# A hybrid attention and long-convolution layer on one core: the short convolution's edge rows in two steps, with zero rows in DRAM, and the first long transform in the order of stored rows

## Chip, cores and metric

The kernel runs on one core of a Trainium2 chip. The metric is the device time of one execution in microseconds (us). The program is written in a tile framework: the Python code issues instructions in some order, a planner in the framework puts the instructions of each engine into a fixed order by priority and by its own estimate of when their inputs are ready (`schedule_with_timeline_sim=True`), and it adds all waits. Each engine, and each queue that issues transfers, then works through its list in order.

## What is computed

One encoder layer, run on two sequences of their own: `s` with 4096 tokens and `p` with 1024, width 1024. Half of the width goes through attention with three dilated windows, the other half through a gated long convolution of order two (hyena).

```python
proj = x @ w_in                              # q, k, v, g_attn: 512 each; u_h: 3 x 512; g_hyena: 512
attn = softmax-weighted sum of three dilated window attentions(q, k, v)
u = b + sum_j pad(u_h)[:, j:j + L] * w[j]    # short convolution, width 3, zero beyond both ends
z = u[..., :C]                               # C = 512
for n in range(2):
    gate = u[..., (n + 1) * C:(n + 2) * C]
    z = gate * (two_sided_fftconv(z, filters[n]) + d[n] * z)
mixed = [rms(attn) * silu(g_attn), rms(z) * silu(g_hyena)]
y = layer_norm(2 ** 0.25 * x + mixed @ w_out)
```

All of it is in float32. Matmuls are made from two-part operands (`h` and `l`, a rounded value and its rest), three products for one.

## The kernel before

Two chains of phases are woven together by `_interleave`. Each phase is a generator that yields the planned cost of the step it has just issued; the chain with the smaller sum goes next. A generator can also yield a name, a flag; its chain then waits until the name is in `self.done`.

- First chain: `proj_first` (u0, u1 and v from x, and x transposed), `proj_second` (u2, q, k), `attention` (which begins with `gate`, the attention's gate projection), `last`, `output`.
- Second chain: `filters` (the long filters and their first transform, into `G`), `convs` (the long convolutions), `hyena` (the hyena gate and the last step of the second convolution).

`proj_first` goes through 40 blocks of 128 tokens, 32 of `s` and 8 of `p`. Block r of a sequence holds the tokens a*R + r for a = 0 to 127, with R = L/128: 32 for `s`, 8 for `p`. So the neighbour of a token is mostly in the block before or after, on the same partition. `short_conv` (lines 416 to 448) takes the projection of one block from PSUM, multiplies it by the three taps, and adds to it what the block before has left. The finished row r - 1 of `u` goes to DRAM when block r is done. Rows 0 and R - 1 lack the contribution that crosses from one partition to the next. Their parts go to a scratch tensor `e` in DRAM (four parts of 128 x 512 for each of u0, u1, u2 of each sequence). A *wrap* finishes one such row: it clears a tile z (L440), loads 127 rows of `e`, shifted by one partition, into it (L441), loads the other part y (L442), adds them on GpSimd (L417) and stores the row of `u` (L444). There are two wraps for each u, twelve in all:

- the four of u0 and u1 of `s` are issued together at the end of block r = 0 of `p` in `proj_first`, then the flag `u_s` is set;
- the four of u0 and u1 of `p` together after the first block of `proj_second`, then the flag `u_p`;
- the two of u2 of `s` at the end of the `s` part of `proj_second`;
- the two of u2 of `p` one by one in `gate`, after steps 270 and 280.

In `proj_first` and `proj_second` the wraps take their two tiles from the tag `m2`, which the projections use too (three buffers in the first, MB = 4 in the second); in `gate` they take the tags kT and qT of attention's own loads.

`convs` runs, in this order: `conv_in(s)` (first transform of u0, into `X`), `conv_mid(s, 0)` (second transform, product with the filter, and back, into `B`), `conv_in(p)`, `conv_out(s)`, `conv_mid(p, 0)`, `conv_mid(s, 1)`, `conv_out(p)`, `conv_mid(p, 1)`. `conv_in` has NB/2 steps (NB = L/64: 32 steps for `s`, 8 for `p`); a step takes the rows n2 and n2 + 1 of `u[0]` seen as NB interleaved rows, in rising order of n2. Such a row n2 lies in the block row n2 mod R. `conv_mid` has NB steps. Its tiles fa and fi have two buffers each, z two, g three, x four. `conv_mid` reads all rows of `X` in every step, so it can't start before `conv_in` has finished.

Transfers are issued from SyncE's queue, all but a few constants (dz, mm, d1), which GpSimd issues. Lines that the prediction uses: L401 the projections' matmuls, L215 three-product matmuls, L478 the transposes of x (into xt; xn is the loaded x), L219 and L227 the rounding and the rest (xh, xl), L425 the stores of `u` and `e`, L663 the stores of `X`, L671 the loads of z in `conv_in`, L711 and L713 the result bo of a step of `conv_mid` and its store, L891 attention's scores, L486 the store of x transposed, L523 the store of v.

```python
m2 = tp.tile([P, C], F32, name="m2")         # a tile of a pool: same name, same ring of buffers
later.append(lambda tp, **k: wrap(tp, 0, slice(0, P - 1), 3, R - 1, **k))
later.append(lambda tp, **k: wrap(tp, 2, slice(1, P), 1, 0, **k))
```

Of the kernel before, what the change touches and what calls it, by code (L numbers as in the profile page):

```python
# [10 lines left out]
F32 = mybir.dt.float32  # L11
# [10 lines left out]
P = 128  # L22
D = 1024
C = 512
# [24 lines left out]
BOOT = 30  # L49
SEQS = (("s", 4096), ("p", 1024))  # L50
# [147 lines left out]
class _Kernel:  # L198
# [31 lines left out]
    def scratch(self, ctx):  # L230
        dp = self.pool(ctx, "dram", 1, DRAM)
        self.S = {}
        for nm, L in SEQS:
            NB = L // N1
            self.S[nm] = dict(
                L=L, NB=NB, A=L // 16,
                x=self.I["x_" + nm],
                R=L // P,
                u=[dp.tile([L, C], F32, name=f"u{i}_" + nm) for i in range(3)],
                e=[dp.tile([4, P, C], F32, name=f"e{i}_" + nm) for i in range(3)],  # L240
                qT=dp.tile([C, L], F32, name="qT_" + nm),
                kT=dp.tile([C, L], F32, name="kT_" + nm),
                v=dp.tile([L, H, VW], BF16, name="v_" + nm),
                o=dp.tile([3, L, H, 66], F32, name="o_" + nm),
                G=[dp.tile([2 * N1, NB, C], F32, name=f"G{i}_" + nm) for i in range(2)],
                X=[dp.tile([2 * N1, NB, C], F32, name=f"X{i}_" + nm) for i in range(2)],
                B=[dp.tile([2 * NB, N1, C], F32, name=f"B{i}_" + nm) for i in range(2)],
                xT=dp.tile([D, L], F32, name="xT_" + nm),
                ga=dp.tile([L, C], F32, name="ga_" + nm),
                mx=dp.tile([L, C], F32, name="mx_" + nm),  # L250
            )

    def globals_(self, ctx):
        nc = self.nc
        gp = self.pool(ctx, "one")
        self.ident = gp.tile([P, P], F32, name="ident")
        with self.tc.high_priority():
            nc.sync.dma_start(out=self.ident, in_=self.I["ident"])
        self.one = gp.tile([P, 1], F32, name="one")
        nc.vector.memset(self.one, 1.0)  # L260


    def filters(self, ctx):
# [151 lines left out]
    def short_conv(self, tp, w, st, nm, i, r, ps, later):  # L415
        nc, S = self.nc, self.S[nm]
        add = lambda o, x: nc.gpsimd.tensor_tensor(out=o, in0=o, in1=x, op=ALU.add)  # L417
        mul = lambda o, x: nc.vector.tensor_tensor(out=o, in0=ps, in1=x, op=ALU.mult)
        R, e = S["R"], S["e"][i]
        ur = S["u"][i].rearrange("(a r) c -> r a c", r=R)  # L420
        n2 = tp.tile([P, C], F32, name="m2")
        mul(n2, w[2])
        if r:
            nc.vector.tensor_tensor(out=n2, in0=n2, in1=st[i][0], op=ALU.add)
        nc.sync.dma_start(out=ur[r - 1] if r > 1 else e[r], in_=n2)  # L425
        t = tp.tile([P, C], F32, name="t0", bufs=3)
        mul(t, w[0])
        a = tp.tile([P, C], F32, name="acc", bufs=2)
        mul(a, w[1])
        add(a, st[i][1] if r else w[3])  # L430
        st[i] = (a, t)
        if r < R - 1:
            add(t, w[3])
            return
        nc.sync.dma_start(out=e[2], in_=t)
        nc.sync.dma_start(out=e[3], in_=a)

        def wrap(tp, src, dst, part, row, tags=("m2", "m2")):
            z, y = (tp.tile([P, C], F32, name=tag) for tag in tags)
            nc.vector.memset(z, 0.0)  # L440
            nc.sync.dma_start(out=z[dst], in_=e[src][slice(1, P) if dst.start == 0 else slice(0, P - 1)])  # L441
            nc.sync.dma_start(out=y, in_=e[part])  # L442
            add(y, z)
            nc.sync.dma_start(out=ur[row], in_=y)  # L444

        later.append(lambda tp, **k: wrap(tp, 0, slice(0, P - 1), 3, R - 1, **k))
        later.append(lambda tp, **k: wrap(tp, 2, slice(1, P), 1, 0, **k))


    def proj_first(self, ctx):  # L450
        nc = self.nc
        xp = self.pool(ctx, "a_x")
        xtp = self.pool(ctx, "a_xt")
        tp = self.pool(ctx, "a_t", 3)
# [4 lines left out]
        work = [(nm, r) for nm, L in SEQS for r in range(L // P)]  # L459
# [39 lines left out]
        st, later = {}, []  # L499
        for b, (nm, r) in enumerate(work):  # L500
            S = self.S[nm]
            for ci in range(3):
# [7 lines left out]
                if ci < 2:  # L510
# [11 lines left out]
                nc.gpsimd.tensor_tensor(out=v2, in0=r1, in1=v1, op=ALU.subtract)  # L522
                nc.sync.dma_start(out=S["v"].rearrange("(a r) h c -> r a (h c)", r=S["R"])[r],  # L523
                                  in_=vt.rearrange("p h c -> p (h c)"))
                if r == 0 and later:
                    for f in later:
                        f(tp)
                    self.done.add("u_" + work[b - 1][0])
                    later.clear()
                yield 5.3  # L530
            cur, nxt = nxt, []
        self.later = later


    def proj_second(self, ctx):
        nc = self.nc
# [36 lines left out]
        for b, (nm, g) in enumerate(work):  # L573
# [11 lines left out]
            for c2 in (2, 3, 0, 1):  # L585
# [24 lines left out]
                        with self.tc.high_priority():  # L610
                            nc.sync.dma_start(out=dst[:, :, c0:c0 + P], in_=qs[:, :, e * P:(e + 1) * P])
                yield 5.3
            if b == 0:
                for f in self.later:
                    f(tp)
                self.done.add("u_" + SEQS[-1][0])
            if last and b < len(work) - 1:
                for f in later:
                    f(tp)
                later.clear()  # L620
            self.later = later
            cur, nxt = nxt, []

        self.done.add("qk")
# [6 lines left out]
    def convs(self, ctx):  # L631
        self.ct = self.pool(ctx, "c_t", 2)
        self.cp = self.pool(ctx, "c_ps", 1, PSUM)
        a, b = (nm for nm, _ in SEQS)
        yield "u_" + a
        yield from self.conv_in(a)
        yield from self.conv_mid(a, 0)
        yield "u_" + b
        yield from self.conv_in(b)
        yield from self.conv_out(a)  # L640
        yield from self.conv_mid(b, 0)
        yield from self.conv_mid(a, 1)
        yield from self.conv_out(b)
        yield from self.conv_mid(b, 1)
        yield "qk"

    def slot(self, name, bufs=2, dt=F32):
# [17 lines left out]
    def conv_in(self, nm):  # L665
        nc, S = self.nc, self.S[nm]
        zr = S["u"][0].rearrange("(m n) c -> n m c", n=S["NB"])
        for n2 in range(0, S["NB"], 2):
            z = self.slot("z", ZB)
            for j in range(2):  # L670
                nc.sync.dma_start(out=z[64 * j:64 * j + 64], in_=zr[n2 + j])  # L671
            self.conv_dft(nm, 0, n2, z)
            yield 2.0

    def conv_mid(self, nm, n):
        nc, S, tp, pp = self.nc, self.S[nm], self.ct, self.cp
        NB = S["NB"]
# [3 lines left out]
        xf = S["X"][n].rearrange("k n c -> (k n) c")  # L681
        gf = S["G"][n].rearrange("k n c -> (k n) c")
        for s in range(NB):
            x = self.slot("x", XB)
            nc.sync.dma_start(out=x, in_=xf[s * P:(s + 1) * P])
            g = self.slot("g", GB)
# [80 lines left out]
    def attention(self, ctx):  # L767
# [79 lines left out]
        with ExitStack() as gx:  # L847
            for i, v in enumerate(self.gate(gx)):
                if i % BOOT == BOOT // 2 and i // BOOT < 9:
                    if i > BOOT:  # L850
                        self.lead = self.last_g
                    load(True)
                    self.lead = None
                if i >= 9 * BOOT and i % 10 == 0 and self.later:
                    self.later.pop(0)(lp, tags=("kT", "qT"))
                yield v
        sp = self.pool(ctx, "t_s", 2)
        pp = self.pool(ctx, "t_ps", 1, PSUM)
# [535 lines left out]
```

## Time and profile before

| | |
|---|---|
| runs | 4416.1, 4419.52, 4421.64 us; median 4419.52 |
| profiled execution | 4421.58 us, span 4419.8 us |
| TensorE matmul | 4038.2 us busy, 91% of the span |
| TensorE weight load | 3416.6 us, 77% |
| VectorE | 3218.0 us, 73% |
| ScalarE | 2152.8 us, 49% |
| GpSimd | 2003.6 us, 45% |
| DMA | 800.87 MB moved, 181 GB/s on average over 16 DMA engines |
| granted TensorE clock, mean | 0.96 |

The profile is of one execution. Its lines give the start and length of an instruction in us, the engine (PE is TensorE's matmul, PEld its weight load, DVE VectorE, ACT ScalarE, POOL GpSimd, SP SyncE; SPq is SyncE's queue, where a long row is an issue that waited), the line of the code, and what is written from what, by the names of tiles (a name like `e_s` is that of a DRAM tensor with its sequence; m is the tile m2, as trailing numbers are left out). In brackets stands how long the engine had been idle and what released it. Rows by stretches give, for one stretch of time, the busy us of each engine with its number of instructions, the granted clock as a share of full speed, the mean busy share of the DMA engines, and GB/s. Rows of groups give the busy us and the mean ns of one instruction, then the idle time ahead of them.

### The profile page before, as it was taken

Reading aid. Unit: us, or ns where it says so; the run is one execution under the profiler, and the core shown is the slowest. Engines: PE = TensorE matmul, PEld = TensorE weight load, DVE = VectorE, ACT = ScalarE, POOL = GpSimd, SP = SyncE. Lnnn points to the kernel's source line nnn. Section 1 sums busy time; section 2 is a strip of 40 time slices with the busy share of each in tenths; the row PEclk is TensorE's granted clock in tenths of the full one; section 3 lists DMA queues with packets and bytes.
Section 4 is the critical chain, followed back from the end, with each engine's and each line's share of the span. In section 5 each row is a group of like instructions: output and inputs, shape, how many; then the busy total and the mean of one; then the engine's idle time right before and its main releaser. Section 6 shows DMA issues by size and latency. Waiting matters only on the chain.

```text
span 4419.8 us, 87947 instructions
## 1 busy us (share of the span) xinstructions
PE 4038.2 (91%) x31996; PEld 3416.6 (77%) x31996; DVE 3218.0 (73%) x6503; ACT 2152.8 (49%) x4246; POOL 2003.6 (45%) x1714
## 2 busy tenths in 40 slices
PE   7999999868789999998989979999999999689897
PEld 6999999858579876887867647888888887477776
DVE  7889888447678754575788666878787877677774
ACT  3433334245344444443465446777777776223332
POOL 4444444335567731366655251414141432266664
PEclk9999999979899999999989988999999999799999
DMA  5555555579555579754566665656565556644441
GB/s 182 180 179 171 178 171 176 178 223 284 166 162 165 165 253 285 230 160 142 170 211 195 215 205 152 175 154 170 155 180 153 153 159 176 217 169 173 173 173 67
DMA packets 662475, 800.87 MB, mean 181 GB/s; under 512 B 68024, under 2 KB 400014, under 8 KB 662042
## 3 DMA queue, kind: packets, MB, share of 16 engines
q1 hardware_dynamic: 643610, 762.64, 55.4%
q0 software_dynamic: 18432, 32.60, 3.2%
q8 instruction: 254, 4.16, 0.4%
q14 instruction: 179, 1.47, 0.1%
HBM read 499.22 MB, written 295.80 MB: 180 GB/s over the span
## 4 chain that ended last, share of the span: by engine, by line
PE 55%; DMA 13%; DVE 10%; POOL 7%; issue 6%; ACT 3%; SPq 2%; POOLq 0%; DVEq 0%; ACTq 0%
PE qk L401 10%; PE u L401 10%; PE pv L950 6%; PE sc L891 5%; PE pt L924 4%; PE g L1182 4%; PE g L1131 3%; POOL hh L1309 2%; DMA oo<-o_s 2%; POOL oo L1271 2%; PE pf L215 2%; PE g L215 2%; PE pz L215 2%; PE c L735 1%; PE c L215 1%
## 5 line engine op out<-in xcount | busy, mean ns | idle before, releaser
L223 POOL TENSOR_SCALAR qc<-q 128x256 fp32r<-128x256 f32 x352 | 246.9, 719 | 707.6 <-PE sc L891 702.0
L401 PE MATMUL u<-wuh,xh 128*128 128x256 f32 x1920 | 556.2, 290 | 10.0 <-ACT wuh L219 9.2
L401 PE MATMUL u<-wul,xh 128*128 128x256 f32 x1920 | 549.1, 286 | 2.2 <-DVE wul L227 2.0
L401 PE MATMUL u<-wuh,xl 128*128 128x256 f32 x1920 | 547.7, 285 | 2.1 <-DVE xl L227 2.1
L227 DVE TENSOR_TENSOR x<-x,xh 128x512 fp32r<-128x512 f32 x320 | 357.7, 1140 | 248.4 <-ACT xh L219 245.6
L915 ACT ACTIVATE sb<-sb,ob 128x192 f32<-128x192 f32 (+2 forms) x960 | 412.2, 473 | 39.9 <-DVE ob L906 31.3
L401 PEld LDWEIGHTS u<-wuh,xh 128*128 128x128 f32 x1920 | 371.6, 194 | 22.8 <-ACT wuh L219 10.4
L401 PEld LDWEIGHTS u<-wul,xh 128*128 128x128 f32 x1920 | 371.8, 194 | 11.9 <-DVE wul L227 3.0
L401 PEld LDWEIGHTS u<-wuh,xl 128*128 128x128 f32 x1920 | 371.4, 193 | 9.9 <-DVE xl L227 2.9
L401 PE MATMUL qk<-xh,wql 128*128 128x256 f32 x1280 | 364.2, 285 | 0.7 <-DVE wql L227 0.5
L401 PE MATMUL qk<-xh,wqh 128*128 128x256 f32 x1280 | 364.4, 285 | 0.0
L401 PE MATMUL qk<-x,wqh 128*128 128x256 f32 x1280 | 364.2, 285 | 0.0
L927 ACT ACTIVATE th<-pt 96x512 f16<-96x512 f32 (+2 forms) x480 | 272.1, 576 | 177.7 <-PE pt L924 174.8
L950 PE MATMUL pv<-V,th 128*128 128x64 bf16 (+3 forms) x5568 | 334.8, 194 | 0.0
L950 PE MATMUL pv<-V,tl 128*128 128x64 bf16 (+3 forms) x3712 | 324.5, 195 | 8.5 <-DVE tl L935 5.4
L935 DVE TENSOR_TENSOR tl<-pt,th 96x512 f16<-96x512 f32 (+2 forms) x480 | 316.2, 667 | 18.8 <-ACT th L927 16.6
L704 POOL TENSOR_TENSOR z<-fa,fi 128x512 f32<-128x512 f32 x160 | 246.2, 1539 | 151.2 <-DVE fi L703 150.5
L227 POOL TENSOR_TENSOR g<-g,gh 128x512 fp32r<-128x512 f32 x160 | 221.1, 1383 | 183.0 <-ACT gh L219 171.4
L219 ACT ACTIVATE xh<-x 128x512 fp32r<-128x512 f32 x400 | 241.9, 633 | 127.4 <-DMA x<-xT_s 42.2
L950 PEld LDWEIGHTS <-th 128*128 128x128 f16 (+1 forms) x5568 | 291.5, 98 | 2.2 <-issue 2.2
L950 PEld LDWEIGHTS <-tl 128*128 128x128 f16 (+1 forms) x3712 | 252.1, 98 | 51.1 <-DVE tl L935 17.6
L924 PE MATMUL pt<-ident,sb 128*128 128x128 f32 (+1 forms) x1856 | 291.1, 283 | 0.3 <-DVE tl L935 0.3
(223 smaller groups left out, 12021.5 us busy)
## 6 DMA issues: line engine op xcount, KB each, us to landing
G_s<-go SPq DMA_DIRECT2D x128, 256.0 KB
g<-G_s SPq DMA_DIRECT2D x128, 256.0 KB
x<-X_s SPq DMA_DIRECT2D x128, 256.0 KB
B_s<-bo SPq DMA_DIRECT2D x128, 256.0 KB
x<-xT_s SPq DMA_DIRECT2D x64, 512.0 KB
oo<-o_s SPq DMA_DIRECT2D x32, 792.0 KB
u_s<-m SPq DMA_DIRECT2D x96, 256.0 KB
V<-v_s SPq DMA_DIRECT2D x168, 145.5 KB
```

The source lines that it names most:

```text
L215: nc.tensor.matmul(out=out, lhsT=l, rhs=r, start=(i == 0), stop=(i == n - 1))
L219: self.nc.scalar.activation(out, in_, AF.Copy, scale=scale)
L223: self.nc.gpsimd.tensor_scalar(out=out, in0=in_, scalar1=scale, scalar2=0.0, op0=ALU.mult, op1=ALU.add)
L227: e.tensor_tensor(out=out, in0=in_, in1=hi.bitcast(F32), op=ALU.subtract)
L401: nc.tensor.matmul(out=out, lhsT=l, rhs=r, start=(k == 0 and i == 0), stop=(k == len(pairs) - 1 and i == len(ops) - 1))
L704: nc.gpsimd.tensor_tensor(out=z, in0=fa, in1=fi, op=ALU.add)
L891: nc.tensor.matmul(out=st["sc"][i], lhsT=qv[half, x], rhs=f(y)[half], start=(j == 0), stop=(j == 2))
L915: nc.scalar.activation(sb[:, i, 0:W], sb[:, i, 0:W], AF.Exp, bias=st["ob"][:, ui, i, 65:66], scale=-1.0)
L924: nc.tensor.transpose(out=pt[0:n, i, t], in_=st["pr"][:, i, t * n:(t + 1) * n], identity=self.ident)
L927: nc.scalar.activation(th[0:n, :, 0:nkt], pt[0:n, :, 0:nkt], AF.Copy)
L935: e.tensor_tensor(out=tl[0:n, :, 0:nkt], in0=pt[0:n, :, 0:nkt], in1=th[0:n, :, 0:nkt], op=ALU.subtract)
L950: last = nc.tensor.matmul(out=pv[:, 0:w], lhsT=st[p][0:n, i, t], rhs=vv[:, VC[b]:VC[b] + w], start=(t == 0 and j == 0), stop=(t == nkt - 1 ...
```

## The change

- `e` gets two more rows in each part, one ahead of and one behind the 128. At the very start a zero tile of 128 x 4 is written to twelve rows of 512 floats in DRAM: the row behind part 0 and the row ahead of part 2, for each of three u and two sequences. The shifted load of a wrap is then 128 whole rows, one of them the zero row, and the clearing of the tile goes.
- A wrap has two steps: `begin` issues the two loads, `end` the add and the store. `wrap_step` first issues the `end` of the wrap begun before, then the `begin` of the next one.
- The four wraps of u0 and u1 of `s` go one by one after blocks r = 0 to 4 of `p` in `proj_first`, with tags of their own (wz, wy, one buffer each). The flag `w_s` is set after block 4.
- All later wraps are taken by whichever comes first, a step of `conv_mid` (tiles from the rings fa and fi) or, in `gate`, every tenth step from 270 on. The flag `w_p` is set by `conv_mid`.
- `conv_in` goes through its rows in the order in which they are stored: first those that need no wrap, each when the flag of its block is set (`u_s4` and so on), then the last four steps, which need `w_s` or `w_p`. The flags `u_s` and `u_p` go.

```diff
@@ -237,7 +237,7 @@
                 x=self.I["x_" + nm],
                 R=L // P,
                 u=[dp.tile([L, C], F32, name=f"u{i}_" + nm) for i in range(3)],
-                e=[dp.tile([4, P, C], F32, name=f"e{i}_" + nm) for i in range(3)],
+                e=[dp.tile([4, P + 2, C], F32, name=f"e{i}_" + nm) for i in range(3)],
                 qT=dp.tile([C, L], F32, name="qT_" + nm),
                 kT=dp.tile([C, L], F32, name="kT_" + nm),
                 v=dp.tile([L, H, VW], BF16, name="v_" + nm),
@@ -258,6 +258,13 @@
             nc.sync.dma_start(out=self.ident, in_=self.I["ident"])
         self.one = gp.tile([P, 1], F32, name="one")
         nc.vector.memset(self.one, 1.0)
+        zero = gp.tile([P, C // P], F32, name="zero")
+        nc.vector.memset(zero, 0.0)
+        for nm, _ in SEQS:
+            for e in self.S[nm]["e"]:
+                for k, row in ((0, P + 1), (2, 0)):
+                    nc.sync.dma_start(out=e[k, row].rearrange("(p f) -> p f", p=P), in_=zero)
+        self.wraps, self.adds = [], []
 
 
     def filters(self, ctx):
@@ -416,7 +423,7 @@
         nc, S = self.nc, self.S[nm]
         add = lambda o, x: nc.gpsimd.tensor_tensor(out=o, in0=o, in1=x, op=ALU.add)
         mul = lambda o, x: nc.vector.tensor_tensor(out=o, in0=ps, in1=x, op=ALU.mult)
-        R, e = S["R"], S["e"][i]
+        R, e = S["R"], [S["e"][i][k, 1:P + 1] for k in range(4)]
         ur = S["u"][i].rearrange("(a r) c -> r a c", r=R)
         n2 = tp.tile([P, C], F32, name="m2")
         mul(n2, w[2])
@@ -435,16 +442,27 @@
         nc.sync.dma_start(out=e[2], in_=t)
         nc.sync.dma_start(out=e[3], in_=a)
 
-        def wrap(tp, src, dst, part, row, tags=("m2", "m2")):
-            z, y = (tp.tile([P, C], F32, name=tag) for tag in tags)
-            nc.vector.memset(z, 0.0)
-            nc.sync.dma_start(out=z[dst], in_=e[src][slice(1, P) if dst.start == 0 else slice(0, P - 1)])
-            nc.sync.dma_start(out=y, in_=e[part])
-            add(y, z)
-            nc.sync.dma_start(out=ur[row], in_=y)
-
-        later.append(lambda tp, **k: wrap(tp, 0, slice(0, P - 1), 3, R - 1, **k))
-        later.append(lambda tp, **k: wrap(tp, 2, slice(1, P), 1, 0, **k))
+        def wrap(src, part, row):
+            def begin(tp, tags, **kw):
+                z, y = (tp.tile([P, C], F32, name=tag, **kw) for tag in tags)
+                nc.sync.dma_start(out=z, in_=src)
+                nc.sync.dma_start(out=y, in_=e[part])
+
+                def end():
+                    add(y, z)
+                    nc.sync.dma_start(out=ur[row], in_=y)
+                return end
+            return begin
+
+        later.append(wrap(S["e"][i][0, 2:P + 2], 3, R - 1))
+        later.append(wrap(S["e"][i][2, 0:P], 1, 0))
+
+    def wrap_step(self, *args, **kw):
+        for f in self.adds:
+            f()
+        self.adds = [f(*args, **kw) for f in self.wraps[:1]]
+        self.wraps = self.wraps[1:]
+        return not self.adds
 
 
     def proj_first(self, ctx):
@@ -522,14 +540,13 @@
                 nc.gpsimd.tensor_tensor(out=v2, in0=r1, in1=v1, op=ALU.subtract)
                 nc.sync.dma_start(out=S["v"].rearrange("(a r) h c -> r a (h c)", r=S["R"])[r],
                                   in_=vt.rearrange("p h c -> p (h c)"))
-                if r == 0 and later:
-                    for f in later:
-                        f(tp)
-                    self.done.add("u_" + work[b - 1][0])
-                    later.clear()
+                if nm != SEQS[0][0] and "w_" + SEQS[0][0] not in self.done and self.wrap_step(tp, ("wz", "wy"), bufs=1):
+                    self.done.add("w_" + SEQS[0][0])
+                if r == S["R"] - 1:
+                    self.wraps, later = later, []
+                self.done.add(f"u_{nm}{r}")
                 yield 5.3
             cur, nxt = nxt, []
-        self.later = later
 
 
     def proj_second(self, ctx):
@@ -610,15 +627,8 @@
                         with self.tc.high_priority():
                             nc.sync.dma_start(out=dst[:, :, c0:c0 + P], in_=qs[:, :, e * P:(e + 1) * P])
                 yield 5.3
-            if b == 0:
-                for f in self.later:
-                    f(tp)
-                self.done.add("u_" + SEQS[-1][0])
-            if last and b < len(work) - 1:
-                for f in later:
-                    f(tp)
-                later.clear()
-            self.later = later
+            if last:
+                self.wraps, later = later, []
             cur, nxt = nxt, []
 
         self.done.add("qk")
@@ -632,16 +642,17 @@
         self.ct = self.pool(ctx, "c_t", 2)
         self.cp = self.pool(ctx, "c_ps", 1, PSUM)
         a, b = (nm for nm, _ in SEQS)
-        yield "u_" + a
         yield from self.conv_in(a)
         yield from self.conv_mid(a, 0)
-        yield "u_" + b
         yield from self.conv_in(b)
         yield from self.conv_out(a)
         yield from self.conv_mid(b, 0)
         yield from self.conv_mid(a, 1)
         yield from self.conv_out(b)
         yield from self.conv_mid(b, 1)
+        for f in self.adds:
+            f()
+        self.adds = []
         yield "qk"
 
     def slot(self, name, bufs=2, dt=F32):
@@ -665,7 +676,12 @@
     def conv_in(self, nm):
         nc, S = self.nc, self.S[nm]
         zr = S["u"][0].rearrange("(m n) c -> n m c", n=S["NB"])
-        for n2 in range(0, S["NB"], 2):
+        R, NB = S["R"], S["NB"]
+        steps = [(f"u_{nm}{r + 2}", n2) for r in range(2, R - 2, 2) for n2 in (r, r + R)]
+        steps += [("w_" + nm, n2) for n2 in (R - 2, NB - 2, 0, R)]
+        for flag, n2 in steps:
+            if flag not in self.done:
+                yield flag
             z = self.slot("z", ZB)
             for j in range(2):
                 nc.sync.dma_start(out=z[64 * j:64 * j + 64], in_=zr[n2 + j])
@@ -681,6 +697,8 @@
         xf = S["X"][n].rearrange("k n c -> (k n) c")
         gf = S["G"][n].rearrange("k n c -> (k n) c")
         for s in range(NB):
+            if self.wrap_step(self.ct, ("fa", "fi"), bufs=2) and f"u_{SEQS[-1][0]}{self.S[SEQS[-1][0]]['R'] - 1}" in self.done:
+                self.done.add("w_" + SEQS[-1][0])
             x = self.slot("x", XB)
             nc.sync.dma_start(out=x, in_=xf[s * P:(s + 1) * P])
             g = self.slot("g", GB)
@@ -851,8 +869,8 @@
                         self.lead = self.last_g
                     load(True)
                     self.lead = None
-                if i >= 9 * BOOT and i % 10 == 0 and self.later:
-                    self.later.pop(0)(lp, tags=("kT", "qT"))
+                if i >= 9 * BOOT and i % 10 == 0:
+                    self.wrap_step(lp, ("kT", "qT"))
                 yield v
         sp = self.pool(ctx, "t_s", 2)
         pp = self.pool(ctx, "t_ps", 1, PSUM)
```

## Prediction

> **What bounds the kernel now.** I read the page first, for the busy shares and the slices, then busy time by stretches wherever the slices dip, then the chain of waits and the queues in order of time inside each dip.
>
> ```profile
> PE 4038.2 (91%) x31996; PEld 3416.6 (77%) x31996; DVE 3218.0 (73%) x6503; ACT 2152.8 (49%) x4246; POOL 2003.6 (45%) x1714
> PE   7999999868789999998989979999999999689897
> ```
>
> TensorE is busy 91% of the span; the next engine, VectorE, 73%. So the time is TensorE's work plus its holes, and a change that moves no matmul can win only in holes. One slice is 110.5 us; there are dips at slices 8 to 11 (884 to 1326 us) and around slices 18 to 23 (1990 to 2650 us). In the first dip SyncE's queue and VectorE, in order of time, show this:
>
> ```profile
> 863.47 3.46 SPq L442 DMA_DIRECT2D m<-e_s  x1
> 867.03 0.54 SPq L523 DMA_DIRECT2D v_p<-vt  x1
> 867.66 0.24 SPq L441 DMA_DIRECT2D m<-e_s  x1
> 878.16 0.33 SPq L444 DMA_DIRECT2D u_s<-m  x1
> ```
>
> ```profile
> 888.85 0.48 DVE L440 MEMSET m<- 128x512 f32 x1 [24.93 <-DMA u_s<-m]
> 889.25 0.63 DVE L227 TENSOR_TENSOR xl<-xt,xh 128x512 fp32r<-128x512 f32 x1
> 903.71 0.48 DVE L440 MEMSET m<- 128x512 f32 x1 [13.83 <-DMA u_s<-m]
> ```
>
> ```profile
> 907.58 1.22 PE L215 MATMUL pz<-gh,dz 128*128 128x512 f32 x2 [35.22 <-DVE gh L227]
> 920.65 0.79 PE L215 MATMUL pz<-gh,dz 128*128 128x512 f32 x1 [11.86 <-ACT fa L662]
> ```
>
> These are the four wraps of the long sequence's u0 and u1: each is a clearing of a tile (L440), two loads from the edge scratch e (L441, L442), an add and a store (L444). They share the tag m2 with the projection's own tiles, so the third and fourth clearing stand on VectorE until an earlier store has landed (24.93 and 13.83 us), and the split xl of the next projection block stands behind them. TensorE gets nothing for 35.22 and again 11.86 us. The chain of waits gives the price of one link:
>
> ```profile
> 867.66 10.50 DMA m<-e_s
> 878.16 10.44 DMA u_s<-m
> ```
>
> Why a 256 KB transfer takes 10 us shows in the DMA rates of another wrap (forty slices of 1985 to 2015 us):
>
> ```profile
> GB/s 224 19 14 22 27 25 25 27 25 27 25 25 27 25 25 27 25 25 87 325 270 142 276 290 385 57 25 25 25 25 27 25 25 25 16 248 385 339 183 377
> ...
> m<-e_s SPq DMA_DIRECT2D x1, 254.0 KB
> ```
>
> For some 10 us the whole core moves 25 GB/s, and then 300. The 254.0 KB load is the L441 one, 127 rows in place of 128: 254 KB / 25 GB/s = 10.2 us. Whole 256 KB transfers show no such plateau, so the 127-row load gets one lane of many, and stores issued behind it finish only after it. By the instructions of line 441 there are 6 + 4 + 2 = 12 of them:
>
> ```profile
> L441 SPq DMA_DIRECT2D m<-e_s x6: 242/247/3702, 862.2 to 1984.7; - x6
> L441 SPq DMA_DIRECT2D m<-e_p x4: 243/268/3652, 1167.3 to 1209.0; - x4
> L441 SPq DMA_DIRECT2D kT<-e_p x2: 242/244/245, 2503.9 to 2529.0; - x2
> ```
>
> They lie in four holes: A at 868 us (four), B at 1168 (four), C at 1988 (two), D at 2510 (two). Busy time by stretches, hole and neighbour:
>
> ```profile
> 868.00:922.00 54.00, 6.92 (x42) 5.80 (x41) 4.77 (x9) 4.08 (x7) 5.60 (x6) 0.57 0.27 85
> 922.00:942.00 20.00, 18.29 (x112) 16.46 (x112) 13.44 (x19) 12.21 (x22) 11.30 (x11) 0.81 0.84 271
> 940.00:1060.00 120.00, 112.04 (x819) 106.33 (x817) 87.82 (x105) 71.26 (x128) 56.53 (x61) 0.98 0.98 302
> 846.00:1085.00 239.00, 181.39 (x1308) 171.41 (x1308) 125.80 (x157) 97.88 (x173) 90.26 (x95) 0.87 0.74 230
> ```
>
> ```profile
> 1168.00:1230.00 62.00, 27.00 (x111) 22.50 (x110) 21.50 (x31) 9.85 (x19) 22.42 (x17) 0.70 0.31 106
> 1240.00:1320.00 80.00, 78.41 (x470) 69.30 (x469) 61.87 (x75) 39.08 (x70) 56.02 (x41) 1.00 0.53 168
> 1988.00:2014.00 26.00, 8.63 (x35) 6.70 (x34) 4.39 (x7) 2.27 (x4) 5.87 (x5) 0.70 0.31 101
> 1970.00:1990.00 20.00, 20.00 (x117) 17.55 (x116) 16.12 (x22) 10.54 (x19) 8.69 (x6) 1.00 0.49 163
> 2510.00:2560.00 50.00, 34.54 (x119) 20.56 (x118) 16.06 (x24) 15.67 (x28) 4.88 (x7) 0.86 0.74 238
> 2480.00:2510.00 30.00, 30.00 (x128) 21.72 (x126) 17.09 (x25) 14.23 (x25) 4.77 (x5) 1.00 0.75 228
> ```
>
> The columns are TensorE, weight load, VectorE, ScalarE and GpSimd busy us (with counts), then granted clock, DMA share, GB/s. I price a hole by its matmuls at the neighbour's pace, since busy time inside a hole counts matmuls at half clock.
>
> **The change, part by part.**
>
> *The wraps' loads become 128 whole rows, the clearing goes, and add and store move to the next step.* Nothing is left on VectorE (12 clearings of 0.48 us; VectorE has room), the slow lane is gone, and tiles have their own tags. I take all four holes as closed.
> A: 54 − 42/(819/120) = 47.9 us; and 922 to 942 us, where the clock is only 0.81, gives 20 − 112/6.83 = 3.6.
> B: 62 − 111/(470/80) = 43.1.
> C: 26 − 35/(117/20) = 20.0.
> D: 50 − 119/(128/30) = 22.1.
> Sum 136.7 us.
> The Trainium skill ("TensorE: Matmul & The Clock Gate", Part 1) says that after an idle window the clock stays at half for about one window of 3.4 us: by that the restart after A costs an estimated 1.7 us, and the sum would be 1.9 us smaller. The row's 0.57 and 0.81 agree in kind; I keep the row's 3.6.
>
> *Conv work starts earlier.* The first transform of the long sequence no longer waits for its wraps: 28 of its 32 steps touch stored rows only. Its loads start at the place of block r=0 of the short sequence (846 us) and not behind hole A. The last four need w_s, given at block r=4. The stretch 846 to 1085 holds eight blocks: (239 − 51)/8 = 23.5 us each, so 28 steps at the old pace (32 in about seven blocks) end near block six: the flag is no new wait. DMA is what is late next: 98% busy at 302 GB/s from 940 to 1060. The stretch moves 239 us × 230 GB/s = 55 MB, at 302 GB/s 182 us, against the 188 us left: just enough, so A's gain stands, with no room beyond it. The conv chain is then about one block, 23 us, ahead of the projections. That pays at the end of the gate, since attention starts only when the conv chain ends:
>
> ```profile
> 2662.38 0.79 PE L215 MATMUL c<-yl,mm 128*128 128x512 f32 x1
> 2663.10 0.53 PE L891 MATMUL sc<-kh,q 64*128 64x192 f32 x2
> ```
>
> Conv steps counted by line 711, in 1240 to 1560 us beside projections, and in 2590 to 2660 alone, with TensorE there:
>
> ```profile
> L711 ACT ACTIVATE bo<-c 128x512 f32<-128x512 f32 x46 | 27.0, 587 | 3.1 <-PE c L215 2.5 <-DMA u_s<-m 0.5
> ```
>
> ```profile
> L711 ACT ACTIVATE bo<-c 128x512 f32<-128x512 f32 x15 | 8.9, 596 | 4.4 <-PE c L215 3.6 <-DMA x<-X_p 0.5
> ```
>
> ```profile
> 2590.00:2660.00 70.00, 45.47 (x123) 24.98 (x121) 52.27 (x69) 37.19 (x65) 55.92 (x43) 0.83 0.63 176
> 0.00:40.00 40.00, 16.01 (x59) 12.10 (x60) 16.46 (x29) 16.92 (x26) 13.68 (x27) 1.00 0.90 287
> ```
>
> A step takes 320/46 = 7.0 us in company, 70/15 = 4.7 alone, and some 2 us of TensorE (8 to 9 matmuls). 23/7.0 = 3.3 steps leave the tail and cost 2 us each elsewhere: 3.3 × 2.7 = 9 us gained. Bounds 0 (nothing shifts) and 40 (all 15 steps: 70 − 30); I take 9.
>
> *New waits.* A wrap's second load may go only when the previous wrap's store has landed (wz and wy have one buffer), and it waits on SyncE's queue; behind it stand the next xn, z and X transfers of that stage, in the mid steps x, g and B. Without the slow lane a transfer's wait in this stretch is:
>
> ```profile
> 977.95 5.40 DMA z<-u_s
> ...
> 1067.11 3.66 DMA X_s<-fi
> ```
>
> Eight of the twelve wraps have a predecessor in their ring: 8 × 4.5 = 36 us if nothing covered it, 0 if the two-deep z and xn buffers do. I take 8, near the cover. In mid steps a wrap borrows one of the two fa and one of the two fi buffers for about eight steps; a step is 7 us and an fa is read within its own step, so 0 to 10 us: I take 3.
>
> *Twelve zero rows at the start.* Each is 128 pieces of 16 bytes, so 96 pieces on each of 16 lanes, in a stretch where DMA is 0.90 busy and TensorE waits for weights. A 2 KB row on the slow lane takes 10.2/127 = 0.08 us; at that price 96 take 7.7 us, at the other end 0, if small pieces are as cheap as those already there, between 3 and 40 us:
>
> ```profile
> DMA packets 7008, 11.32 MB, mean 306 GB/s; under 512 B 1182, under 2 KB 2292, under 8 KB 7008
> ```
>
> I take 4. The Trainium skill ("DMA: Bandwidth & Descriptors", Specifications) says that writes below 512 B are read, modified and written back. No run here shows one; as a doubling of the row's price, by my estimate, that is 15 us, and the sum would give 4302.
>
> Sum: −136.7 − 9 + 8 + 3 + 4 = −131. The profiled execution took 4421.6 us (span 4419.8), 2 us above the median of the runs: 4421.6 − 131 = 4291.
>
> **The rivals.**
>
> 1. *The wait moves to SyncE's queue.* The same eight holds are uncovered, each 4.5 us and a slow restart of 3.6: 65 us in place of 8, 4348. For it: the stretch is DMA-bound, so landings are slowest there, and every load and store of both chains is on this one queue. Against: z and xn are two deep, x four.
> 2. *The tail goes entirely.* If the conv chain gains 100 us on the projections in place of 23, 40 us are won for 9: 4260. For it: conv steps are far behind their place, 15 of them alone at the end. Against: TensorE is full between the holes, so the planner has no free place for them.
> 3. *Slower, by the zero rows.* They stand ahead of the weights at the start. They decide from 131/96 = 1.4 us for one 16-byte write on a lane; at 1.5 us the time is 4291 − 4 + 144 = 4431. Against: 17 times the row's price for 2 KB, and 1182 small pieces pass beside 306 GB/s.
> 4. *It doesn't do what it says:* the shifted load of 128 rows still goes at 25 GB/s, the adds and stores wait for it as before and only the clearing is off VectorE: about 4420. Against: L442's loads of the same scratch are whole and show no plateau of their own.
>
> **How the numbers follow.** The sum's case 0.66, rival 1 0.17, rival 2 0.08, rival 3 0.04, rival 4 0.05. A change under 0.2% can't be told from none. Faster: 0.66 + 0.17 + 0.08 = 0.91; same 0.05; slower 0.04. The likeliest's own range is 4265 (no new costs, 20 us from the tail) to 4330 (36 us of holds, 7.7 at the start, 10 in the rings). The range for 8 in 10 goes from 4255, under rival 2, to 4360, over rival 1.
>
> **What would show it.** Right: no stretch of 25 GB/s at the wraps; line 440's clearing gone and xl no longer behind it; TensorE's longest idle between 840 and 1250 us under 10 us; first attention matmul near 2663 − 137 − 9 = 2517 us; TensorE busy time near 4038 less the half-clock parts. Wrong: SyncE rows of several us at the wraps' second load, with TensorE idle behind; a first projection matmul later by over 10 us; conv steps alone before attention for more than 70 us, which would mean that the flag at block four holds the chain.

## The result, and the profile after

The changed kernel took 4301.41 us (median of 4 runs, 4298.37 to 4310.77) against 4417.81 us (4 runs) for the kernel before: ratio 0.9741, 95% interval 0.9722 to 0.9760. The forecast was 4291, range 4255 to 4360. The profiled execution took 4300.97 us, its span is 4299.2 us, 120.6 us shorter than the span before; the medians differ by 116.4, as the profiled execution before was among its slowest. All times here are those of executions at the usual clock; one of `e4_old_order`, 5736.61 us at a granted clock of 0.627, is left out.

Engine shares and slices from the page of the changed kernel:

```profile
PE 4010.9 (93%) x31996; PEld 3403.2 (79%) x31996; DVE 3210.6 (75%) x6492; ACT 2156.7 (50%) x4246; POOL 1998.5 (46%) x1714
PE   6999999998999999999899879999999998689987
```

The same 31996 matmuls; TensorE is busy 27 us less, at a mean granted clock of 0.971 in place of 0.96. The dip at slices 8 to 11 is gone. The DMA rates around the first four wraps (forty slices of 852 to 932 us), and the wraps' second loads:

```profile
GB/s 140 203 267 285 357 261 284 356 368 303 320 329 318 389 401 362 390 304 345 391 371 318 345 293 417 253 356 341 290 372 334 177 280 381 400 327 365 344 297 358
```

```profile
L449 SPq DMA_DIRECT2D wy<-e_s x4: 325/523/617, 856.5 to 912.6; - x4
L449 SPq DMA_DIRECT2D fi<-e_s x2: 319/351/383, 2446.4 to 2459.1; - x2
```

No plateau at 25 GB/s, and no issue of a wrap's second load took longer than 0.617 us (duration in ns, least, median, greatest): SyncE's queue did not stand there. TensorE's longest idle time between 840 and 1250 us is 4.5 us, before 35.2. Busy time where the holes were, and in the stretch before attention (columns as before):

```profile
852.00:1018.00 166.00, 164.91 (x1252) 158.08 (x1251) 118.81 (x143) 95.39 (x167) 86.95 (x93) 1.00 1.00 317
1120.00:1160.00 40.00, 38.69 (x257) 35.05 (x255) 28.99 (x35) 16.80 (x31) 31.46 (x24) 1.00 0.75 237
2370.00:2400.00 30.00, 27.57 (x112) 20.54 (x111) 14.51 (x21) 10.86 (x19) 7.96 (x7) 0.94 0.75 223
2448.00:2538.00 90.00, 54.12 (x141) 30.05 (x140) 58.61 (x81) 43.20 (x76) 66.83 (x51) 0.78 0.65 184
```

The first three are the places of the wraps of u0 and u1 of `s`, of `p`, and of u2 of `p`: TensorE is busy 99, 97 and 92%, in the first with the DMA engines full. The two wraps of u2 of `s`, before at 1988 us, are now issued at the head of the fourth stretch (2446.4 and 2459.1 us in the rows above). This stretch is the *tail*, from the gate's last store to attention's first score: TensorE does conv steps alone there, is 60% busy at clock 0.78, and the tail is longer than before. Where the 120.6 us come from is read from a few rows, first and last start of each group (the row that begins with a time is the issue of the first loads of `conv_mid(p, 1)`, the conv chain's last phase):

```profile
L342 SPq DMA_DIRECT2D G_p<-go x32: 319/320/455, 705.9 to 852.5; - x32
L703 SPq DMA_DIRECT2D x<-X_s x128: 319/382/1516, 1017.9 to 2329.2; - x128
L703 SPq DMA_DIRECT2D x<-X_p x32: 319/366/630, 1717.4 to 2508.3; - x32
2450.76 0.79 SPq L703 DMA_DIRECT2D x<-X_p  x2
L1158 SPq DMA_DIRECT2D ga_p<-wst x8: 319/320/473, 2397.7 to 2448.4; - x8
L909 PE MATMUL sc<-kh,q x512: 245/293/580, 2538.8 to 3257.6; 64*128 64x256 f32 x160, 64*128 64x192 f32 x11
```

Their like before:

```profile
L335 SPq DMA_DIRECT2D G_p<-go x32: 319/320/455, 699.1 to 846.0; - x32
L685 SPq DMA_DIRECT2D x<-X_s x128: 319/383/1938, 1070.9 to 2435.3; - x128
L685 SPq DMA_DIRECT2D x<-X_p x32: 319/370/2762, 1809.0 to 2633.2; - x32
2570.36 4.19 SPq L685 DMA_DIRECT2D x<-X_p  x4
L1140 SPq DMA_DIRECT2D ga_p<-wst x8: 319/358/1585, 2524.2 to 2587.2; - x8
L891 PE MATMUL sc<-kh,q x512: 245/290/579, 2663.1 to 3377.8; 64*128 64x256 f32 x160, 64*128 64x192 f32 x11
```

| us from the start of the span | before | after | moved forward by |
|---|---|---|---|
| last filter row stored (G_p) | 846.0 | 852.5 | −6.5 |
| second transform's first load (x<-X_s) | 1070.9 | 1017.9 | 53.0 |
| first load of `conv_mid(p, 0)` (x<-X_p) | 1809.0 | 1717.4 | 91.6 |
| first load of `conv_mid(p, 1)` (x<-X_p) | 2570.4 | 2450.8 | 119.6 |
| gate's last store (ga_p) | 2587.2 | 2448.4 | 138.8 |
| attention's first score (sc) | 2663.1 | 2538.8 | 124.3 |
| end | 4419.8 | 4299.2 | 120.6 |

From the filters' end to the first score 130.8 us were won (124.3 + 6.5); 6.5 were lost before that, 3.7 after it. The first chain (projections, gate) won 138.8, more than the score, so the tail grew from 75.9 to 90.4 us. It holds the same number of conv steps as the prediction counted before, 15; they are `conv_mid(p, 1)`, all but the last of its 16:

```profile
L729 ACT ACTIVATE bo<-c 128x512 f32<-128x512 f32 x15 | 8.9, 594 | 5.7 <-PE c L215 5.7
```

That phase is not slower: from its first load to the first score it takes 88.0 us, before 92.7.

### The profile page after: what moved, and what is told of

Its sections match the earlier page's. It is cut to its first block, busy times and chain, and to the rows that moved or that the text cites. A ratio compares the mean times of both kernels' runs of the same rounds, so it can differ in the third digit from the quotient of the medians.

```text
span 4299.2 us, 87919 instructions
## 1 busy us (share of the span) xinstructions
PE 4010.9 (93%) x31996; PEld 3403.2 (79%) x31996; DVE 3210.6 (75%) x6492; ACT 2156.7 (50%) x4246; POOL 1998.5 (46%) x1714
```

## The experiments

The edits are shortened; `...` stands for lines left out.

**Whole rows alone, and two steps alone.** Theory 1: the one-lane load is the cost. Theory 2: the deferral pays. `e1_rows` puts the zero rows and the wide load into the kernel before; `e2_steps127` puts the old load into the changed kernel.

```diff
 # e1_rows, on the kernel before (and e with P + 2 rows, the twelve zero rows)
-            nc.vector.memset(z, 0.0)
-            nc.sync.dma_start(out=z[dst], in_=e[src][slice(1, P) if dst.start == 0 else slice(0, P - 1)])
+            nc.sync.dma_start(out=z, in_=S["e"][i][0, 2:P + 2] if dst.start == 0 else S["e"][i][2, 0:P])
 # e2_steps127, on the changed kernel (no zero rows)
-                nc.sync.dma_start(out=z, in_=src)
+                nc.vector.memset(z, 0.0)
+                nc.sync.dma_start(out=z[dst], in_=src)        # 127 rows
 ...
```

> The kernel before, with the zero rows in DRAM and the shifted load as 128 whole rows (no clearing); the wraps stay in one step, four together, in tag m2, and conv_in keeps its order and flags. Theory 1 (the one-lane load is most of the cost): each of the twelve wraps loses its 10 us load, but the four together still go through three m2 buffers one behind the other, load 2.5 + add 1.3 + store 2.5 us each. The holes shrink from 136 to some 50 us: 85 us gained, 6 lost at the start for the zero rows: about 4340, no stretch of 25 GB/s. Theory 2 (the deferral is what pays, not the lane): at most the clearing's share, 4400 to 4425.

> The changed kernel with the old load: the tile is cleared and 127 shifted rows are loaded into it, no zero rows in DRAM; two steps, new tags, new order of conv_in stay. Theory 1: the loads are off VectorE's path, but the lane is still blocked for 10 us twelve times, and all transfers with a part on that lane behind it; in the first stretch, DMA-bound at 300 GB/s, four of them cost up to 40 us, in the mid steps and the gate another 20 to 40 us; the start gains 6: about 4350, with plateaus of 25 GB/s. Theory 2 (deferral alone is enough): 4290 to 4300, the plateaus harmless.

Whole rows alone: 4315.79 us, 0.9771 (0.9756 to 0.9786) of the kernel before, so 101 of the change's 116 us. Two steps, new tags and the new order with 127 rows: 4405.79, 0.9977 (0.9967 to 0.9986), 11 us. The load is the cost, more strongly than theory 1 had it: it gave 4340 for the first run, which came out 24 us lower, and 4350 for the second, which came out 56 us higher. Even four wraps in one step leave little, and deferral alone gains little. In `e1_rows`, at the first four wraps and at the next four:

```profile
870.00:910.00 40.00, 28.37 (x186) 25.89 (x185) 17.74 (x22) 14.26 (x25) 15.09 (x15) 0.79 0.73 230
1130.00:1200.00 70.00, 68.99 (x407) 60.73 (x406) 57.06 (x68) 35.76 (x64) 55.52 (x39) 1.00 0.68 221
```

Of hole A some 12 us and a slower clock are left, of hole B next to nothing. In `e2_steps127` the plateaus stand where the wraps are (850 to 930 us), and the chain of waits has the shifted load itself:

```profile
GB/s 281 299 37 25 261 236 283 111 25 107 340 284 237 311 270 341 209 56 305 353 256 25 203 192 295 339 326 78 49 256 309 347 29 25 160 320 312 204 404 317
```

```profile
850.51 17.58 DMA wz<-e_s
```

**Is it 127, or any load that does not fill the tile?** `e5_split` is the changed kernel without zero rows; the tile is cleared and the 127 rows come in two loads.

```diff
-                nc.sync.dma_start(out=z, in_=src)
+                nc.vector.memset(z, 0.0)
+                for r0, n in ((0, 112), (112, 15)):
+                    nc.sync.dma_start(out=z[d0 + r0:d0 + r0 + n], in_=src[r0:r0 + n])
 ...
```

> The changed kernel without zero rows: the tile is cleared and the 127 shifted rows come in two loads, of 112 and of 15 rows. Two steps, tags and order as in the changed kernel. Theory 1 (127 rows go on one lane because 127 has no divisor up to 16; 112 rows use 16 lanes, 15 rows 15): no plateau of 25 GB/s, and without the zero-row stores at the start the filters end near 846 and the time is 4294 to 4300. Rival (any load that begins off the first partition or row, or does not fill the tile, is slow): as the kernel with 127 rows and two steps, about 4400.

4289.10 us, 0.9709 (0.9691 to 0.9726). The same 127 rows, off the first partition and not filling the tile, in two loads cost nothing, so the rival is out: it is the count of rows in one transfer. (The time is 5 us below theory 1's range.) The Trainium skill ("DMA: Bandwidth & Descriptors", Why a DMA increments its semaphore by 16 and not by 1) says that a transfer is spread over the largest number of engines up to 16 that divides the slowest dimension of both its sides, here its row count, and that 127 rows go over one. The runs agree: 254 KB at 25 GB/s with 127 rows, no plateau of some 10 us with 128, or with 112 and 15.

**The start.** The filters end 6.5 us later. Four runs move or reshape the twelve stores.

```diff
 # e6_zero_256: 8 pieces of 256 bytes a row, in place of 128 of 16
+        zero = gp.tile([P, 64], F32, name="zero")
 ...
+                    nc.sync.dma_start(out=e[k, row].rearrange("(p f) -> p f", p=8), in_=zero[0:8])
 # e3_zero_late: the stores issued in proj_first, one a block
+                if b >= 4 and self.zrows:
+                    nc.sync.dma_start(out=self.zrows.pop(0), in_=self.zero)
 ...
 # e8_zero_held: as e3 from block 16, and the zero tile made from block 15's data
+                    nc.vector.tensor_scalar(out=self.zero, in0=r1[...], scalar1=0.0, scalar2=0.0, op0=ALU.mult, op1=ALU.add)
 ...
 # e10_zero_act: nc.scalar.dma_start in place of nc.sync.dma_start
```

> The changed kernel, with the twelve zero-row stores issued one at a time from block 4 of proj_first on, in place of at the very start. Theory 1 (the 6.5 us that the filters end later come from the 16-byte stores standing among the first weight loads): the last store of G_p comes near 846 us again and the time falls by 5 to 7 us, to about 4295. Rival (another order of the instructions at the start, not the stores): no change, 4301.

> The changed kernel with each zero row stored as 8 pieces of 256 bytes in place of 128 pieces of 16 bytes: 96 pieces in place of 1536. Theory 1 (the filters end 6.5 us later because the 16-byte pieces hold the queue and the lanes while the weights load): SyncE's row of 7.23 us for five stores becomes about 2, the filters end at 846 to 848, the time falls by 4 to 7 us to about 4296. Rival (the twelve more issues, or another order at the start): filters near 852, 4301.

> The changed kernel with the zero tile made only after block 15 of proj_first (from that block's data times zero), so that the twelve stores of 16-byte pieces can't be issued before some 400 us, one at a block. Theory 1 (they cost because they stand among the first weights): the filters end near 846 to 848, 4294 to 4298. Rival (16-byte stores cost their 6 us of lane or queue time wherever they stand): the filters end near 852 all the same, 4301.

> The changed kernel with the twelve zero-row stores (16-byte pieces, at the start) issued from ScalarE's queue and not from SyncE's. Theory 1 (what they cost is their place in SyncE's queue ahead of the weights and the filters' constants): the first weight load is issued near 5 us again, the filters end at 846 to 849, about 4290. Theory 2 (the transfers themselves hold the DMA engines in the loaded first 40 us, from whichever queue): the filters end near 852, 4299 to 4303.

| | time, us | ratio to before | filters end, us | stores issued, us |
|---|---|---|---|---|
| changed kernel | 4301.41 | 0.9741 (0.9722 to 0.9760) | 852.5 | 3.6 to 22.2 |
| e3_zero_late | 4300.46 | 0.9737 (0.9719 to 0.9755) | 852.4 | 27.3 to 46.7 |
| e6_zero_256 | 4299.30 | 0.9742 (0.9729 to 0.9756) | 853.0 | 3.6 to 18.8 |
| e8_zero_held | 4287.39 | 0.9713 (0.9699 to 0.9726) | 846.8 | 450.8 to 460.7 |
| e10_zero_act | 4296.38 | 0.9730 (0.9717 to 0.9743) | 850.4 | 0.9 to 17.2 |

`e3_zero_late` did not do what it was meant to: the planner drew the stores forward to 27 us, among the filters' constants, and nothing changed. `e8_zero_held`, whose data forbids that, has the filters' end back at 846.8, and 14 us of the time. With a sixteenth of the pieces nothing changed, so piece size is not it; the place in the first 47 us is. All the runs bear this out: with the stores issued in the first 47 us the filters end at 850.4 to 857.5 us, without them (`before`, `e2_steps127`, `e5_split`, `e8_zero_held`, `e9_split_cf06`, `e11_split_cf04`) at 846.0 to 848.8. SyncE's queue of the changed kernel, and the first six stores by their own durations:

```profile
7.18 7.23 SPq L266 DMA_DIRECT2D e_s<-zero  x5
14.52 0.38 SPq L485 DMA_DIRECT2D xn<-x_s  x1
15.34 0.32 SPq L266 DMA_DIRECT2D e_p<-zero  x1
16.04 0.33 SPq L397 DMA_DIRECT2D t<-w_in  x1
```

```profile
L266 SPq DMA_DIRECT2D e_s<-zero x6: 319/526/963, 3.6 to 14.1; - x6
```

The row of five is a stretch of 7.23 us with nothing else in it, not one long issue: no store took longer than 0.963 us to issue, and they stand up to 2.8 us apart. The first load of projection weights goes at 16.04 us, before at 4.91. Still it is not the projections that lose by it; their first matmul comes as before, but the filters' first one comes 13.8 us later. Before, then after:

```profile
24.16 0.58 PE L401 MATMUL u<-wuh,xh 128*128 128x256 f32 x1 [6.76 <-ACT wuh L219]
26.94 1.19 PE L301 MATMUL tap<-mc,w 66*128 66x512 f32 x1 [0.40 <-DMA mc<-zf_s]
```

```profile
24.24 0.58 PE L408 MATMUL u<-wuh,xh 128*128 128x256 f32 x1 [6.99 <-ACT wuh L219]
40.76 0.59 PE L308 MATMUL tap<-mc,w 66*128 66x512 f32 x1
```

From ScalarE's queue the stores held ScalarE instead (two rows of 5.12 and 9.13 us, its first activation after them), and the filters ended in between. Whether the queue, the transfers or the planner's other order of the loads sets the 6.5 us stays open, and so does how the 5.7 us that `e8_zero_held` wins at the filters' end become 14 at the end.

**The conv chain's place.** `e4_old_order` lets all of `conv_in` wait for w_s; `e7_cf06` issues the conv chain's steps earlier; `e9_split_cf06` and `e11_split_cf04` do that with the split load.

```diff
 # e4_old_order
-        steps = [(f"u_{nm}{r + 2}", n2) for r in range(2, R - 2, 2) for n2 in (r, r + R)]
-        steps += [("w_" + nm, n2) for n2 in (R - 2, NB - 2, 0, R)]
+        steps = [("w_" + nm, n2) for n2 in range(0, NB, 2)]
 # e7_cf06, e9_split_cf06 (0.6), e11_split_cf04 (0.4); wraps not yet taken are kept
-FF, CF, GF = 2.4, 0.8, 3.2
+FF, CF, GF = 2.4, 0.6, 3.2
```

> The changed kernel with conv_in's rows in rising order again, so that all its steps wait for w_s (block 4 of p) or w_p. Theory 1 (the conv chain's end gates attention, and its steps alone cost 4.7 us for 2 us of TensorE): the chain starts some 90 us later, some 13 steps move into the tail at 2.7 us each: 35 us slower than the changed kernel, about 4335, the tail from the gate's last store to the first score 30 to 60 us longer than its 90. Theory 2 (the planner fills the gap with projections and the tail does not depend on the start): 4300 to 4305.

> The changed kernel with the planned cost of the conv chain's steps at 0.6 in place of 0.8 of their figures, so they are issued earlier among the projections (and wraps not yet taken are kept when new ones are added). Theory A (the place in the issue order sets how far the conv chain gets before the gate ends): the chain ends earlier against the gate, the 90 us tail shrinks by 30 to 60 us, 2.7 us gained for each 4.7 us step: 4265 to 4285. Theory B (conv steps already stand ahead of their turn, their pace is set by TensorE's in-order share and their own latencies): no change, 4297 to 4305, tail 80 to 95 us.

> The split load (112 and 15 rows, no zero rows) together with the conv chain's steps issued earlier (planned cost 0.6 of their figure). Theory (two separate effects: the start, some 12 us with the split, and the place of the conv chain, some 17): they add up, the filters end near 847, attention's first score comes some 12 us ahead of the 2521 of the kernel with 0.6 alone, about 4272. Rival (both act on the same tail before attention, so one takes what the other would): 4282 to 4290.

> As the kernel with the split load and 0.6, with the planned cost at 0.4. Theory A (place sets the pace of the conv chain): the tail before attention shrinks again by 10 to 20 us, 4255 to 4265. Theory B (the conv steps already stand as early as their own latencies let them, 0.6 took what was there): within 5 us of the kernel with 0.6.

`e4_old_order`: 4340.24 us, 0.9822 (0.9806 to 0.9838), 39 us slower than the changed kernel. Its second transform starts at 1115.9 us, 98 us later; its gate ends 28 us earlier, at 2420.0; its first score comes 36.5 us later, at 2575.3. Attention does wait for the conv chain, as theory 1 has it, and of the 98 us of lateness 36.5 are left at the first score. But its 35 us came out of thirteen steps more in the tail at 2.7 us each, and the tail, 155.3 us long, holds six more (21 in place of 15): that the time agrees is luck, and no run shows the 2.7 us. This run also tells what the two steps cost without the new order: it is 24 us slower than `e1_rows`, and its second transform starts 80 us later, as `w_s` is set after block 4 and the flag `u_s` of `e1_rows` after block 0. `e7_cf06`: 4284.56, 0.9706 (0.9692 to 0.9719): place does matter, by 17 us, at the edge of theory A; but the tail shrank by 13 us, to 77.2, where that theory had 30 to 60. Its profiled run has the first score at 2521.5. `e9_split_cf06` (4289.90, 0.9708) and `e11_split_cf04` (4287.42, 0.9706) are no better than either part: the effects don't add up, and 0.4 finds no more than 0.6. All three have their first score between 2521 and 2528 us, and so have `e5_split` and `e8_zero_held`; in all five `conv_mid(p, 1)` loads first at 2429.6 to 2433.8 us and takes 91.9 to 94.9 us from there. Why it starts just there stays open.

**Are the two steps needed?** `e12_one_step` is `e1_rows` (wraps four together, in m2) with `conv_in` in the order of stored rows.

```diff
-        yield "u_" + a          # and the same for b
+        steps = [(f"u_{nm}{r + 2}", n2) for r in range(2, R - 2, 2) for n2 in (r, r + R)]
+        steps += [("u_" + nm, n2) for n2 in (R - 2, NB - 2, 0, R)]
 ...
```

> The kernel before with the zero rows and the 128-row load (wraps in one step, four together, in tag m2) and with conv_in in the order of stored rows, its last four steps waiting for the wraps. What is missing against the changed kernel is only the two steps and their own tags. Theory 1 (the two steps are worth nothing once the load is wide; what is left between the whole rows alone, 4316, and the changed kernel, 4301, is the earlier start of the conv chain): 4295 to 4304. Rival (the one-step wraps still leave a hole on VectorE and TensorE of some 12 us at the first four, and that is the difference): 4310 to 4318.

4295.40 us, 0.9720 (0.9703 to 0.9737): no slower than the changed kernel, though a hole of the rival's size is there, 12 us idle in 870 to 910 us:

```profile
870.00:910.00 40.00, 28.16 (x156) 22.41 (x154) 15.48 (x23) 24.41 (x43) 11.31 (x16) 0.77 1.08 359
852.00:1018.00 166.00, 149.10 (x1052) 137.31 (x1052) 103.30 (x129) 92.75 (x165) 77.31 (x85) 0.93 1.00 316
```

In the whole stretch that is 16 us of TensorE's busy time and 200 matmuls less than in the changed kernel, at the same full DMA (its filters end 3.9 us later, which is part of it). The gate ends 34 us later (2482.9), but the second transform starts at 1010.6 and the first score comes at 2535.9, 3 us earlier. What the hole takes from the projections is free, as attention waits for the conv chain anyway. So the two steps and their own tags, a part of the change, bought nothing that these runs can tell; the wide rows and the order do it. Against `e1_rows` the order alone is worth 20 us.

## Why the prediction was right, and where it was off

*The cause.* Twelve 127-row loads, some 10 us each on one lane (25 GB/s, where 300 is usual): shown by `e1_rows` (101 us), `e2_steps127` and `e5_split`. Rival 4 (the shifted load stays slow) is out.

*The holes, 136.7 us.* They are closed: where the wraps of A, B and D now stand TensorE is 99, 97 and 92% busy, and at C none stands any more. But the sum took every hole as time on one line of work. After the change two chains end at attention, and the first score moved with the conv chain: 130.8 us from the filters' end, against 134.7 by the same terms (136.7 + 9 − 8 − 3). From the table, counted from the filters' end, the conv chain won 59.5 us up to its second transform (hole A: 51.5), 38.6 from there to `conv_mid(p, 0)` (hole B: 43.1), and 32.7 from there to the first score (holes C and D: 42.1). So the total is right in part by luck: the chain won 8 us more than hole A, 14 less than the other three, and 9 of the tail and 11 of new waits did not come. That the projections' part of hole A counts is not right either: `e12_one_step` leaves part of it open and loses nothing.

*"The conv chain is then about one block, 23 us, ahead", and 3.3 steps leave the tail.* This step failed, with its 9 us. At the second transform the chain was 8 us ahead (59.5 against 51.5), not 23. The block-wise pace was taken as the conv chain's, but in that stretch, with the projections beside it, the DMA engines are full (1.00 busy at 317 GB/s); that this sets its pace is likely, but no run shows it. And no step left the tail: the 15 steps counted there are the conv chain's last phase, which can begin only when the phase before it has stored all of `X_p`; the same 15 are there after the change. The gate's last store moved forward by 138.8 us, the start of that phase by 119.6, so the tail grew by 14.5 us where it should have shrunk. Rival 2 (the tail goes entirely) is out. The prediction's own sign of being wrong, conv steps alone before attention for more than 70 us, came true with 90.4, though not for the reason given there, the flag. That a late conv chain costs was right: `e4_old_order` came out 39 us slower. The price of 2.7 us a step is not shown.

*The first score near 2517.* This left out the sum's own 8, 3 and 4 us; with them it is 2532, and the score came at 2538.8.

*New waits, 8 and 3.* Too dear: no wrap's load held SyncE's queue (0.617 us at most); at the mid steps' wraps of `p` TensorE is 97% busy, and the phase that has the wraps of u2 of `s` is no longer than before (88.0 us against 92.7). Rival 1 is out. *The flag at block 4* was no wait: the last of its stores was issued at 920.97 us, the last row of `X` some 94 us later.

*The zero rows, 4.* 6.5 at the filters' end, and some 14 of the time by `e8_zero_held`. The bound by pieces (0 to 7.7 us) was built on the wrong quantity: with a sixteenth of the pieces the filters end no earlier. Rival 3 named the right place and a price ten times too high; the first projection matmul, its sign, did not move (24.16 and 24.24 us). The Trainium skill's rule on writes below 512 bytes ("DMA: Bandwidth & Descriptors", Specifications) is not decided by this: the pieces of `e6_zero_256` are still below that size, and no run stored larger ones.

The remaining 3.7 us lie behind the first score, where nothing was changed. Over all fourteen profiles that stretch takes 1752.3 to 1764.0 us (1756.7 before, 1760.4 after), so they tell nothing of the change. The forecast was some 10 us low: 3.9 from holes, tail and waits together (134.7 against 130.8), 2.5 at the start, 3.7 behind the first score.

## To carry to other kernels

Look at the DMA rate inside a stall. Here a plateau at 25 GB/s beside the usual 300 was one transfer that was not spread, and the row count of that transfer (127 against 128, or 112 and 15) decided it. Before moving a wait off an engine, see whether the thing waited for can be made short; here that alone gave 101 of 116 us, and with the early start of the conv chain the rest (`e12_one_step`). Where two chains meet, price each hole on the chain that arrives last, and see whether the steps at its end are a phase that can't begin earlier.

## What was not expected of the hardware

Twelve transfers of 2 KB each, issued in the first 22 us beside the weight loads, put off the filters' first matmul by 13.8 us and cost some 12 to 14 us of the whole (`e5_split` and `e8_zero_held` against the changed kernel), in 1536 pieces or in 96. With the conv steps issued earlier no such cost shows: `e7_cf06` has the transfers, `e9_split_cf06` has not, and it is no faster (4289.90 against 4284.56). The fastest versions seen are `e7_cf06` (4284.56), `e8_zero_held` (4287.39) and, without zero rows at all, `e11_split_cf04` and `e5_split` (4287.42 and 4289.10); the intervals do not tell them apart.
